# Rotary by halves: columns of the query and key weights reordered, halves exchanged out of PSUM by ScalarE, row copies issued by GpSimd

## The chip, the cores and the metric

The kernel runs on one core of one Trainium2 chip. The core has five engines that run at the same time, each with its own instruction queue, taken in order: TensorE (PE: matmuls from SBUF into PSUM), VectorE (DVE), ScalarE (ACT), GpSimd (POOL) and SyncE (SP, which here only issues DMAs). The metric is the device time of one execution in microseconds; lower is better.

## What is computed

Two layers over 512 positions of width 1024, all in float32. Each layer has a mixer of three branches (a convolution with 31 taps, a short gated convolution, a differential attention with rotary) and an MLP of width 4096, each behind an RMS norm that is modulated by a conditioning vector. The change concerns the queries and keys of the attention alone:

```python
def apply_rope(t, cos, sin):
    t1, t2 = jnp.split(t, 2, axis=-1)
    return jnp.concatenate([t1 * cos - t2 * sin, t2 * cos + t1 * sin], axis=-1)

q = apply_rope(q.reshape(bsz, seq, N_HEADS, 2, HEAD_DIM), cos, sin)
k = apply_rope(k.reshape(bsz, seq, N_HEADS, 2, HEAD_DIM), cos, sin)
...
s = jnp.einsum('bqhcd,bkhcd->bhcqk', qb, kb).astype(jnp.float32) * scale
p = jax.nn.softmax(jnp.where(mask, s, -jnp.inf), axis=-1)
a = p[:, :, 0] - lam * p[:, :, 1]
```

There are 8 heads, each with two components of 64 channels. In each component, channel i (of the first 32) and channel i + 32 are turned together. The scores of the two components go through separate softmaxes.

## The kernel before

**Numbers.** Every float32 operand of a matmul is split into a high part (rounded to TensorE's float32r type) and a low part (the rest). A product is three passes: high by high, high by low, low by high (`PASSES`, line 415). A weight chunk of 1024 x 128 is split by `w_split` (line 371): ScalarE casts the high part (line 394), one step later VectorE subtracts it from the raw weights (line 402). Raw weights come in tiles of 1024 x 256 (1 MB) on SP's queue (line 367); there are two raw tiles, so the next load is issued when a tile's second chunk has been split.

**Layout.** Activations are transposed: 128 channels on the partitions, 512 positions along the row. One `product` (line 426) is 24 matmuls of 512 columns (8 parts of the contraction, 3 passes) into one PSUM bank. For queries and keys such a product holds one head: 128 rows, component 0 in rows 0 to 63, component 1 in rows 64 to 127, and in each component the first half of the channels and then the second.

**The order of the work.** The program writes the order of all engines' instructions itself. A clock advances by one step for every 4096 columns that matmuls of the large products stream (`mm`, line 143: eight matmuls of 512 columns). Side work is written as generators: `yield n` hands back until n steps later, and `spawn` puts a generator on the heap. Whatever a generator emits lands, in that order, in the queues of its engines, behind all that was emitted before.

**A head pair.** In each layer the mixer makes four pairs of heads, each of four products (query and key of one head, query and key of the next), followed by the values of the two heads. After each of the four products `rope` (line 707) is spawned with no delay. `heads` (in `mixer`) starts head after head: each 9 steps after the one before, and not before its rotated query and key are there; the first head waits 2 more steps (`FIRST`). `attend` (line 780) then forms the scores (lines 789 and 790) in four groups, two steps apart, into two PSUM banks, each group needing the banks that the group before filled; the softmax's first VectorE instruction (line 754) empties them. Later it transposes, multiplies with the values, and forms a small norm on POOL (lines 834 to 836 and 438) whose result TensorE spreads over the rows (line 455).

**The rotation.** `rope` copies the product out of PSUM (ScalarE, line 712), and four DMAs on SP's queue copy 32 rows each, so that the tile `sw` holds every half in the place of the other (line 714). VectorE multiplies the copy by the cosines (717), `sw` by the signed sines (719), and adds (720). The sum is cast to d0 and d1 (ScalarE, 723 and 724). For the query (j even) VectorE makes the low parts e0 and e1 (728, 729); for the key it makes the low part in place (734). Then DMAs on SP's queue copy rows, 64 at a time (738, 739), so that for each component there is a tile with 128 contraction rows: for the query the high part twice and the low part twice, for the key the high part and the low part. `RWAIT` is the number of steps from those DMAs to the moment when the head may use the result.

**The start.** The first pair's four products run at the start, by quarters of the contraction while weights arrive. Their order is written out by hand in `START`: `h` casts a quarter of a weight chunk on ScalarE (line 1270), `l` subtracts on VectorE (line 1276), `m` modulates two parts of the input, `p` is a quarter of a product. p12 to p15 are the last quarters of the four products, and each spawns its `rope` (`first_product`). l13 is the low part of the weights that p13 uses; h16 and l16 split the first chunk of the values. In the second layer the first three of the four products are formed at the end of `closing`, between the halves of the layer before.

Of the kernel before, what the change touches and what calls it, by code (L numbers as in the profile page):

```python
# [43 lines left out]
CPACE, ADA0, ADA1, APACE = 0.71, 2.36, 2.19, 1.62  # L44
ADA_BR = 0
FIRST = 2
RWAIT = 2


RDELAY = (0, 1, 1)  # L50
# [21 lines left out]
def kernel(  # L72
# [31 lines left out]
    def ftile(dt=F32, shape=None):  # L104
        return slot("f", dt, shape)
# [245 lines left out]
        return s  # L351


    specs, chunks = [], []
    for l in range(L):
        for sp in wspecs(l):
            grp = sp if isinstance(sp[0], tuple) else (sp,)
            chunks += [(len(specs) + g, hh) for hh in range(2) for g in range(len(grp))]
            specs += grp
    raws, wready = [], []  # L360
# [2 lines left out]
    def raw_issue():  # L363
        if len(raws) < len(specs):
            src, c0, kk = specs[len(raws)]
            raw = wraw.tile([P, 8, 256], F32, tag="raw", name=nm("raw"))
            nc.sync.dma_start(raw[:, : abs(kk), :],
                              src[:, c0 : c0 + 256].rearrange("(k p) e -> p k e", p=P))
            raws.append(raw)

    def w_split(extra=None):


        if wnext[0] >= len(chunks):
            return
        n, hh = chunks[wnext[0]]
        wnext[0] += 1
        raw, kk = raws[n], specs[n][2]
        if kk < 0:

            shape, rs = [P, 4, 256], raw[:, 4 * hh : 4 * hh + 4, :]
            n_k = 4
        else:
            shape, rs = [P, 8, P], raw[:, :kk, hh * P : (hh + 1) * P]
            n_k = kk
        if extra:
            half = [P, n_k // 2] + shape[2:]
            his = [slot(extra, F32R, half) for _ in range(2)]
            parts = [(hf, rs[:, i * half[1] : (i + 1) * half[1], :]) for i, hf in enumerate(his)]
        else:  # L390
            hi = wpool.tile(shape, F32R, tag="wh", name=nm("wh"))
            parts = [(hi[:, :n_k, :], rs)]
        for h_, r_ in parts:
            A.copy(h_, r_)  # L394
        yield 1
        if extra:
            los = [slot(extra, F32R, half) for _ in range(2)]
        else:
            lo = wpool.tile(shape, F32R, tag="wl", name=nm("wl"))
            los = [lo[:, :n_k, :]]  # L400
        for l_, (h_, r_) in zip(los, parts):
            V.tensor_tensor(l_, r_, h_.bitcast(F32), op=ALU.subtract)  # L402
        wready.append(([h_[:, k, :] for h_, _ in parts for k in range(n_k // len(parts))],
                       [l_[:, k, :] for l_ in los for k in range(n_k // len(parts))], extra))
        if hh == 1:
            raw_issue()
# [300 lines left out]
    def rope(pp, res, j):  # L707

        t, sw = ftile(), ftile()
        A.copy(t, pp)
        for q in range(4):
            nc.sync.dma_start(sw[32 * q : 32 * q + 32, :], t[32 * (q ^ 1) : 32 * (q ^ 1) + 32, :])  # L714
        yield 1
        u = ftile()
        V.tensor_tensor(u, t, cos_t, op=ALU.mult)
        yield 2
        V.tensor_tensor(sw, sw, sin_t, op=ALU.mult)  # L719
        V.tensor_tensor(u, u, sw, op=ALU.add)  # L720
        yield 1
        d0, d1 = slot("qk", F32R), slot("qk", F32R)
        A.copy(d0, u)
        A.copy(d1[64:, :], u[64:, :])
        yield 1
        if j % 2 == 0:
            e0, e1 = slot("qk", F32R), slot("qk", F32R)
            V.tensor_tensor(e0, u, d0.bitcast(F32), op=ALU.subtract)
            V.tensor_tensor(e1[64:, :], u[64:, :], d1[64:, :].bitcast(F32), op=ALU.subtract)
            moves = ((d0, d0, d1, d1), (e0, e0, e1, e1))  # L730
            parts = (d0, d1, e0, e1)
        else:
            lo = u.bitcast(F32R)
            V.tensor_tensor(lo, u, d0.bitcast(F32), op=ALU.subtract)
            moves = ((d0, u, d1, u),)
            parts = (d0, d1)
        for a0, b0, a1, b1 in moves:
            nc.sync.dma_start(a0[64:, :].bitcast(F32), b0[:64, :].bitcast(F32))
            nc.sync.dma_start(a1[:64, :].bitcast(F32), b1[64:, :].bitcast(F32))
        yield RWAIT  # L740
        res.append(parts)

# [403 lines left out]
    def angles():  # L1146
# [15 lines left out]
        for t in (ang, n_):  # L1162
            V.tensor_scalar(out=t, in0=t, scalar1=PI, scalar2=-PI, op0=ALU.min, op1=ALU.max)
        yield
        A.activation(sin_t, ang, AF.Sin, scale=rc[:, 1:2])
        A.activation(cos_t, n_, AF.Sin)

# [97 lines left out]
    def high(n):  # L1265
        if n == 16:
            w_tasks.append(w_split("cv"))
            next(w_tasks[0])
        else:
            A.copy(w_quarter(n, 0), raw_quarter(n))  # L1270

    def low(n):
        if n == 16:
            next(w_tasks[0], None)
        else:
            V.tensor_tensor(w_quarter(n, 1), raw_quarter(n), w_quarter(n, 0).bitcast(F32), op=ALU.subtract)
            if n // 4 == 3 and n % 4 > 1:
                raw_issue()

# [98 lines left out]
```

## Time and profile before

| | |
|---|---|
| median of 3 runs | 1906.89 us (1906.71 to 1907.18) |
| the profiled execution | 1904.28 us, of which 1902.5 us is the span from the first to the last instruction |
| TensorE busy | 1874.3 us, 99% of the span |
| VectorE, ScalarE, POOL busy | 1256.0, 785.8 and 63.4 us |
| granted TensorE clock, mean | 0.997 |
| DMA | 241.20 MB, mean 127 GB/s |

Line numbers such as L714 are those of the kernel before. A group's row gives the line, the engine, the operation, the tiles it writes and reads, and the number of instructions; then the busy time, the mean duration, and how long the engine stood idle just before them and on whom. A timeline's row gives the start in the span, the duration, and in brackets the idle time before it and what ended it. Matmuls overlap, and their ends are modelled: the time from one start to the next is the better measure of TensorE. The first layer's attention runs from about 55 to 300 us, the second's from about 985 to 1215 us.

### The profile page before, as it was taken

To read this page: it belongs to the slowest core of one execution; us is meant where nothing else is said; L and a number is where in the kernel's file an instruction comes from. 1 tells how busy PE (TensorE), PEld (TensorE's weight loads), DVE (VectorE), ACT (ScalarE), POOL (GpSimd) and SP (SyncE) were. 2 spreads that over 40 slices of the span, in tenths; PEclk is the share of its full clock that TensorE was granted. 3 is DMA by queue.
4 is the path that set the end of the run, shared out by engine and by line. 5 is a ranking of instruction groups with operands and counts; after the bars stand their busy time and mean duration, and the time that the engine had idled before them with its cause. 6 is when DMAs were issued, how large, how long until landed. Compare 5 with 4: busy or idle time off the path is not lost.

```text
span 1902.5 us, 24972 instructions
## 1 busy us (share of the span) xinstructions
PE 1874.3 (99%) x9565; PEld 1599.9 (84%) x9565; DVE 1256.0 (66%) x2139; ACT 785.8 (41%) x1420; POOL 63.4 (3%) x109
## 2 busy tenths in 40 slices
PE   8999999999999999999999999999999999999998
PEld 6788888888889888888898888888888898888888
DVE  7788789996676556565677777898654563333336
ACT  4466652223333524333445666322243353424253
POOL 1011010000000000000000000000000000000000
PEclk9999999999999999999999999999999999999999
DMA  8644323444554455555535442232233422223221
GB/s 272 181 130 126 101 67 98 151 138 145 166 178 135 139 178 195 177 185 182 171 97 142 123 122 73 89 104 96 67 100 100 133 89 89 89 93 106 89 89 67
DMA packets 211527, 241.20 MB, mean 127 GB/s; under 512 B 10408, under 2 KB 178480, under 8 KB 211408
## 3 DMA queue, kind: packets, MB, share of 16 engines
q1 hardware_dynamic: 210480, 239.38, 40.6%
q8 instruction: 75, 1.23, 0.3%
q0 software_dynamic: 768, 0.23, 0.1%
q14 instruction: 44, 0.36, 0.1%
q10 hardware_dynamic: 160, 0.01, 0.0%
HBM read 216.50 MB, written 2.10 MB: 115 GB/s over the span
## 4 chain that ended last, share of the span: by engine, by line
PE 93%; DMA 3%; DVE 2%; issue 1%; SPq 1%; ACT 1%; POOL 0%; POOLq 0%; DVEq 0%; ACTq 0%
PE mm L145 83%; PE s L145 3%; DMA f<-f 2%; PE t L817 1%; PE s L789 1%; PE s L790 1%; PE t L806 1%; SPq L714 1%; PE t L1193 1%; PE t L455 0%; PE t L303 0%; PE t L825 0%; POOL st L438 0%; DVE f L719 0%; PE t L1214 0%
## 5 line engine op out<-in xcount | busy, mean ns | idle before, releaser
L145 PE MATMUL mm<-h,wh 128*128 128x512 f32 x2720 | 851.3, 392 | 0.0
L145 PEld LDWEIGHTS mm<-h,wh 128*128 128x128 f32 x2720 | 509.6, 188 | 103.3
L145 PE MATMUL mm<-h,wl 128*128 128x512 f32 x1360 | 533.6, 392 | 0.0
L394 ACT CAST wh<-raw 128x1024 fp32r<-128x1024 f32 (+1 forms) x308 | 308.9, 1005 | 407.2 <-PE mm L145 358.2
L402 DVE TENSOR_TENSOR wl<-raw,wh 128x1024 fp32r<-128x1024 f32 (+1 forms) x308 | 358.2, 1166 | 69.6 <-ACT wh L394 65.9
L145 PE MATMUL mm<-qk,wh 128*128 128x512 f32 (+1 forms) x1024 | 300.2, 376 | 0.0
L145 PEld LDWEIGHTS mm<-h,wl 128*128 128x128 f32 x1360 | 256.2, 188 | 51.9
L145 PEld LDWEIGHTS mm<-qk,wh 128*128 128x128 f32 x1024 | 188.2, 188 | 35.1
L145 PE MATMUL mm<-qk,wl 128*128 128x512 f32 (+1 forms) x512 | 192.6, 376 | 0.0
L912 DVE SCALAR_TENSOR_TENSOR cv<-v,caw,cv 128x511 f32<-128x511 f32 (+14 forms) x240 | 176.0, 733 | 4.2
L499 DVE SCALAR_TENSOR_TENSOR xT<-mm,ada,xT 128x512 f32<-128x512 f32 (+1 forms) x81 | 56.0, 691 | 151.2 <-PE mm L145 151.0
L281 DVE SCALAR_TENSOR_TENSOR araw<-araw,cact,araw 128x512 f32<-128x512 f32 x140 | 104.6, 747 | 25.2 <-DMA araw<-in_w_ada_dram 24.7
L145 PEld LDWEIGHTS mm<-qk,wl 128*128 128x128 f32 x512 | 96.3, 188 | 17.2
L1059 ACT ACTIVATE f<-mm 128x512 f32<-128x512 f32 x60 | 35.9, 598 | 160.6 <-PE mm L145 160.6
L145 PE MATMUL mm<-o,wh 128*128 128x512 f32 (+1 forms) x320 | 95.5, 381 | 0.0
L145 PE MATMUL mm<-v,wh 128*128 128x512 f32 (+1 forms) x320 | 94.9, 379 | 0.0
L145 PE MATMUL mm<-wh,h 128*128 128x256 f32 x448 | 84.1, 284 | 0.0
L761 ACT ACTIVATE cv<-cv,st 128x128 f32<-128x128 f32 (+3 forms) x128 | 71.0, 558 | 25.6 <-DVE st L754 25.2
L1033 DVE SCALAR_TENSOR_TENSOR f<-f,mm 128x512 f32<-128x512 f32 x38 | 26.1, 687 | 83.6 <-PE mm L145 83.6
L469 DVE TENSOR_TENSOR qk<-f,qk 128x512 fp32r<-128x512 f32 x38 | 26.3, 691 | 77.4 <-ACT qk L466 77.2
L438 POOL TENSOR_TENSOR st<-st,nhalf 128x4 f32<-128x4 f32 (+2 forms) x29 | 31.2, 1076 | 1368.0 <-DVE st L460 1013.4
L145 PEld LDWEIGHTS mm<-wh,h 128*128 128x128 f32 x448 | 70.8, 191 | 0.4
(259 smaller groups left out, 2282.9 us busy)
## 6 DMA issues: line engine op xcount, KB each, us to landing
raw<-in_w_in_dram SPq DMA_DIRECT2D x66, 1024.0 KB, 5.2
raw<-in_w_ff_dram SPq DMA_DIRECT2D x64, 1024.0 KB, 5.4
araw<-in_w_ada_dram SPq DMA_DIRECT2D x160, 256.0 KB, 3.0
f<-f SPq DMA_DIRECT2D x128, 64.0 KB, 2.0
qk<-qk SPq DMA_DIRECT2D x64, 128.0 KB, 2.6
raw<-in_w_c_out_dram SPq DMA_DIRECT2D x8, 1024.0 KB, 5.0
raw<-in_w_out_dram SPq DMA_DIRECT2D x8, 1024.0 KB, 5.0
qk<-in_w_ada_dram SPq DMA_DIRECT2D x16, 256.0 KB, 6.0
```

What stands on the lines that cost most here:

```text
L145: T.matmul(ps, lhsT, rhs, start=start, stop=stop)
L281: V.scalar_tensor_tensor(out=part, in0=r, scalar=cact[:, k : k + 1], in1=part, op0=ALU.mult, op1=ALU.add)
L394: A.copy(h_, r_)
L402: V.tensor_tensor(l_, r_, h_.bitcast(F32), op=ALU.subtract)
L438: G.tensor_tensor(y, v[:, :n], nhalf[:, :n], op=ALU.pow)
L469: V.tensor_tensor(lo, src, hi.bitcast(F32), op=ALU.subtract)
L499: V.scalar_tensor_tensor(out=xT[e][:, t0:t1], in0=pp[:, t0:t1], scalar=g[:, e : e + 1], in1=xT[e][:, t0:t1], op0=ALU.mult, op1=ALU.add)
L714: nc.sync.dma_start(sw[32 * q : 32 * q + 32, :], t[32 * (q ^ 1) : 32 * (q ^ 1) + 32, :])
L761: A.activation(p[cc][:, :n], p[cc][:, :n], AF.Exp, bias=nb[:, cc : cc + 1], scale=-1.0, accum_out=l0[:, i : i + 1] if cc == 0 else s1)
L912: V.scalar_tensor_tensor(out=ac[:, s:], in0=glu[j][:, : S - s], scalar=wk, in1=ac[:, s:], op0=ALU.mult, op1=ALU.add)
L1033: V.scalar_tensor_tensor(out=t, in0=t, scalar=1.0, in1=pp, op0=ALU.add, op1=ALU.mult)
L1059: A.activation(r, pp, AF.Relu)
```

## The change

1. The columns of the query and key weights are put in another order as they are split: for each head first the 32 first-half channels of component 0, those of component 1, then the second halves of both. Each cast and each subtraction of such a chunk becomes two instructions over half the columns (`turn_high`, `turn_low`), at the start too.
2. A product then holds all first halves in rows 0 to 63 and all second halves in rows 64 to 127. Two ScalarE copies of 64 rows, straight out of PSUM, put the halves in each other's place; the four exchange DMAs are gone. VectorE multiplies by the cosines straight out of PSUM, in the rope's first step.
3. The sign of the sines follows: the first 64 rows get -1, the others 1 (two small `memset`s).
4. d1 and e1 are made over all 128 rows.
5. The row copies move 32 rows at a time, twice as many of them, on GpSimd's DMA queue.
6. The waits between the rope's steps were 1, 2, 1, 1 and `RWAIT` = 2; they are 1, 1, 1 and `RWAIT` = 3.

```diff
-RWAIT = 2
+RWAIT = 3
...
-    specs, chunks = [], []
+    specs, chunks, turned = [], [], set()
     for l in range(L):
         for sp in wspecs(l):
             grp = sp if isinstance(sp[0], tuple) else (sp,)
+            if len(grp) > 1 and grp[0][1] in range(2560, 3584):
+                turned.update(range(len(specs), len(specs) + 2))
...
+    def by_half(w):
+        v = w.rearrange("p k (c s f) -> p k s c f", c=2, s=2)
+        return [v[:, :, i] for i in range(2)]
+
+    def by_part(w):
+        v = w.rearrange("p k (s c f) -> p k s c f", c=2, s=2)
+        return [v[:, :, i] for i in range(2)]
+
+    def turn_high(hi, raw):
+        for a, b in zip(by_part(hi), by_half(raw)):
+            A.copy(a, b)
+
+    def turn_low(lo, raw, hi):
+        for a, b, c_ in zip(by_part(lo), by_half(raw), by_part(hi.bitcast(F32))):
+            V.tensor_tensor(a, b, c_, op=ALU.subtract)
...
+        turn = kk > 0 and n in turned
         for h_, r_ in parts:
-            A.copy(h_, r_)
+            if turn:
+                turn_high(h_, r_)
+            else:
+                A.copy(h_, r_)
...
-            V.tensor_tensor(l_, r_, h_.bitcast(F32), op=ALU.subtract)
+            if turn:
+                turn_low(l_, r_, h_)
+            else:
+                V.tensor_tensor(l_, r_, h_.bitcast(F32), op=ALU.subtract)
...
-        t, sw = ftile(), ftile()
-        A.copy(t, pp)
-        for q in range(4):
-            nc.sync.dma_start(sw[32 * q : 32 * q + 32, :], t[32 * (q ^ 1) : 32 * (q ^ 1) + 32, :])
-        yield 1
-        u = ftile()
-        V.tensor_tensor(u, t, cos_t, op=ALU.mult)
-        yield 2
+        sw, u = ftile(), ftile()
+        A.copy(sw[:64, :], pp[64:, :])
+        A.copy(sw[64:, :], pp[:64, :])
+        V.tensor_tensor(u, pp, cos_t, op=ALU.mult)
+        yield 1
         V.tensor_tensor(sw, sw, sin_t, op=ALU.mult)
         V.tensor_tensor(u, u, sw, op=ALU.add)
         yield 1
         d0, d1 = slot("qk", F32R), slot("qk", F32R)
         A.copy(d0, u)
-        A.copy(d1[64:, :], u[64:, :])
+        A.copy(d1, u)
         yield 1
         if j % 2 == 0:
             e0, e1 = slot("qk", F32R), slot("qk", F32R)
             V.tensor_tensor(e0, u, d0.bitcast(F32), op=ALU.subtract)
-            V.tensor_tensor(e1[64:, :], u[64:, :], d1[64:, :].bitcast(F32), op=ALU.subtract)
+            V.tensor_tensor(e1, u, d1.bitcast(F32), op=ALU.subtract)
...
         for a0, b0, a1, b1 in moves:
-            nc.sync.dma_start(a0[64:, :].bitcast(F32), b0[:64, :].bitcast(F32))
-            nc.sync.dma_start(a1[:64, :].bitcast(F32), b1[64:, :].bitcast(F32))
+            for r in (0, 64):
+                G.dma_start(a0[r + 32 : r + 64, :].bitcast(F32), b0[r : r + 32, :].bitcast(F32))
+                G.dma_start(a1[r : r + 32, :].bitcast(F32), b1[r + 32 : r + 64, :].bitcast(F32))
         yield RWAIT
         res.append(parts)
...
+        V.memset(rc[:64, 1:2], -1.0)
+        V.memset(rc[64:, 1:2], 1.0)
         A.activation(sin_t, ang, AF.Sin, scale=rc[:, 1:2])
...
-            A.copy(w_quarter(n, 0), raw_quarter(n))
+            turn_high(w_quarter(n, 0), raw_quarter(n))
...
-            V.tensor_tensor(w_quarter(n, 1), raw_quarter(n), w_quarter(n, 0).bitcast(F32), op=ALU.subtract)
+            turn_low(w_quarter(n, 1), raw_quarter(n), w_quarter(n, 0))
```

## The prediction

> **What bounds the kernel now.** The page comes first: the span, the engines, and the DMA issues by kind.
>
> ```profile
> span 1902.5 us, 24972 instructions
> ...
> PE 1874.3 (99%) x9565; PEld 1599.9 (84%) x9565; DVE 1256.0 (66%) x2139; ACT 785.8 (41%) x1420; POOL 63.4 (3%) x109
> ...
> f<-f SPq DMA_DIRECT2D x128, 64.0 KB, 2.0
> ```
>
> TensorE fills 99% of the span. The change takes no matmul away, so it can only give back moments in which TensorE stands still or runs slowly, and it can only cost by making new ones. The second view is therefore TensorE's table of waits (who, on whom: total, times, longest).
>
> ```profile
> PE s L789 <- DVE st L754: 5.6, 5, 2.2
> PE s L789 <- DMA qk<-f: 3.4, 2, 3.2
> ```
>
> L789 forms the scores, so the first two rows are attention's: scores wait five times for a bank that the softmax's first VectorE instruction (L754) must empty, and twice for the keys' row copies. The 3.2 us one is layer 0's first head. The timeline of TensorE shows what it costs beyond the wait, and the table by stretches shows the granted clock there (0.91).
>
> ```profile
> 72.29 0.61 PE L145 MATMUL mm<-h,wh 128*128 128x512 f32 x2
> 76.10 0.30 PE L789 MATMUL s<-qk,qk 128*128 128x128 f32 x1 [3.19 <-DMA qk<-f]
> ...
> 77.11 0.73 PE L145 MATMUL mm<-h,wl 128*128 128x512 f32 x1
> ...
> 80.06 0.62 PE L145 MATMUL mm<-h,wh 128*128 128x512 f32 x2
> ...
> 82.13 0.28 PE L789 MATMUL s<-qk,qk 128*128 128x256 f32 x1
> ...
> 82.60 0.63 PE L145 MATMUL mm<-h,wh 128*128 128x512 f32 x2
> ```
>
> ```profile
> 60.00:80.00 20.00, 15.92 (x103) 14.39 (x102) 14.79 (x29) 10.59 (x20) 0.56 (x1) 0.91 0.63 165
> ...
> 100.00:120.00 20.00, 18.25 (x133) 16.71 (x132) 18.28 (x46) 13.52 (x30) 1.59 (x4) 1.00 0.48 126
> ```
>
> Nine matmuls lie between 80.06 and 82.13: 0.23 us each. The seven between 77.11 and 80.06 took 2.95 instead of 1.61 us, and four score matmuls took 1.01 us (76.10 to 77.11), against 0.47 for four larger ones at 82.13. So this wait cost 3.19 + 1.34 + 0.54 = 5.07 us.
>
> Why do the five others wait? The chain of waits passes, shortly before each of them, through an exchange of halves, the copy f<-f of L714:
>
> ```profile
> 91.51 5.96 DMA f<-f
> ...
> 106.11 4.63 DMA f<-f
> ...
> 1020.23 5.99 DMA f<-f
> ...
> 1067.28 6.15 DMA f<-f
> ...
> 1114.42 6.68 DMA f<-f
> ```
>
> The page's median landing is 2.0 us; these took 4.6 to 6.7, on the queue that also carries the 1 MB weight loads. VectorE takes its instructions in order: its product with the sine (L719) stands waiting for the exchange, L754 is queued behind, and TensorE waits for L754.
>
> **The change, part by part.** Unit costs, from the groups between 60 and 310 us (busy us, mean ns, then idle):
>
> ```profile
> L723 ACT CAST qk<-f 128x512 fp32r<-128x512 f32 x16 | 9.9, 621 | 12.2 <-DVE f L720 6.5 <-PE s L789 5.6
> L724 ACT CAST qk<-f 64x512 fp32r<-64x512 f32 x16 | 9.9, 618 | 0.3
> ...
> L717 DVE TENSOR_TENSOR f<-f,cos_t 128x512 f32<-128x512 f32 x14 | 9.6, 685 | 0.0
> ...
> L712 ACT COPY f<-mm 128x512 f32<-128x512 f32 x13 | 7.5, 580 | 14.3 <-PE mm L145 14.2
> ...
> L991 DVE TENSOR_TENSOR f<-f,mm 128x512 f32<-128x512 f32 x2 | 1.4, 684 | 1.0 <-PE mm L145 1.0
> ...
> L908 DVE TENSOR_SCALAR cv<-v,caw,prm 128x512 f32<-128x512 f32 x2 | 1.1, 542 | 0.0
> ...
> L994 DVE TENSOR_SCALAR f<-f,prm 128x512 f32<-128x512 f32 x2 | 1.0, 480 | 0.0
> ```
>
> 1. *The exchange goes* (128 DMAs on SP's queue). Two ScalarE copies of 64 rows out of PSUM replace one of 128. Rows do not set the price (L724 with 64 costs what L723 does with 128), so this adds one 0.58 us copy per rope on an engine that is 41% busy; d1 and e1 over all rows are free by the same two rows. The cosine product reads PSUM, which costs VectorE nothing more (L991 against L717). With no exchange to wait for, the five L754 waits have lost their cause: **gain 5.6 us**. No row shows what is late next; the bounds are 0 (something else holds VectorE equally long) and 5.6, and I take all and charge new lateness in part 5.
>
> 2. *Halved weight casts and subtractions.* VectorE's cost shows where the program already cuts a 1024-column split in two (55.09 against 57.22); ScalarE's is bounded by two casts like L723 against one of 1024 columns:
>
> ```profile
> 65.61 1.05 ACT L394 CAST wh<-raw 128x1024 fp32r<-128x1024 f32 x1 [3.54 <-DMA raw<-in_w_in_dram]
> ```
>
> ```profile
> 39.83 0.35 DVE L1183 TENSOR_SCALAR part<-v,cact 128x256 f32<-128x256 f32 x1
> ...
> 51.74 0.42 DVE L1276 TENSOR_TENSOR wl<-raw,wh 128x256 fp32r<-128x256 f32 x1
> ...
> 55.09 1.29 DVE L402 TENSOR_TENSOR cv<-raw,cv 128x512 fp32r<-128x512 f32 x2
> ...
> 57.22 1.15 DVE L402 TENSOR_TENSOR wl<-raw,wh 128x1024 fp32r<-128x1024 f32 x1
> ...
> 66.69 1.22 DVE L402 TENSOR_TENSOR wl<-raw,wh 128x1024 fp32r<-128x1024 f32 x1 [2.07 <-ACT wh L394]
> ...
> 72.53 0.69 DVE L734 TENSOR_TENSOR f<-f,qk 128x512 fp32r<-128x512 f32 x1
> ```
>
> That is +0.19 us on ScalarE (2 × 0.62 − 1.05) and +0.14 on VectorE per chunk, 2 to 3 us of each over a layer's 16 chunks, covered by their free shares. Runs of 32 columns have no row. Lower bound 0; upper bound doubled (+1.2 us per chunk on VectorE), which would feed the second rival. I take the low end, since today's casts already read runs of 128 out of rows of 256 at about one column per ns. At the start there is no such cover: between the rows at 39.83 and 51.74 VectorE's timeline has no pause, and six quarter subtractions (L1276) stand ahead of the last modulation. Six times 0.14: **loss 0.8 us**; bounds 0 and 15 × 0.14 = 2.1.
>
> 3. *The cosine product moves ahead of l13.* The start list runs "p12 l13 h16 p13". The rope's first step now puts a VectorE instruction, waiting for p12's last matmul, in front of l13, the low part of the weights of p13, whose third matmul needs it.
>
> ```profile
> 53.39 0.39 PE L145 MATMUL mm<-h,wl 128*128 128x512 f32 x1
> ...
> 54.07 0.39 PE L145 MATMUL s<-h,wl 128*128 128x512 f32 x1
> ```
>
> p12 ends at 53.8. Then 0.69 (product) and about 0.5 (l13 in halves): l13 is ready at 55.0 instead of 52.2, and p13's third matmul, at 54.07 now, waits about 1.0 us with the semaphore's way: a new wait. **Loss 1.1 us**; bounds 0.5 (l13 alone) and 1.6 (with slow running in the proportion 5.07 to 3.19).
>
> 4. *Row copies on POOL, twice as many, half as large; the head starts one step (8 matmuls, 1.85 us) earlier*, because the waits inside a rope fall from seven steps to six. What POOL's issues cost and how long such a copy takes:
>
> ```profile
> 118.92 0.53 POOL L204 DMA_DIRECT2D f<-in_b_ada_dram  x1 [16.25 <-PE t L221]
> ...
> 120.29 1.29 POOL L835 TENSOR_SCALAR st<-st 128x4 f32<-128x4 f32 x1
> ...
> 159.84 0.22 POOL L835 TENSOR_SCALAR st<-st 128x4 f32<-128x4 f32 x1
> ```
>
> ```profile
> f<-in_conv_a_w_dram POOLq DMA_DIRECT2D x2, 62.0 KB, 2.5
> ```
>
> A query rope issues 8 × 0.53 = 4.2 us, a key rope 2.1 us. Queued behind them on POOL are the head's small norm (L834 to L438) and a few parameter loads; the norm is wanted only steps later, so I charge nothing. SP loses all its rope work, and with it a block: in the start its next weight load stands behind eight exchange issues,
>
> ```profile
> 59.87 0.53 SPq L367 DMA_DIRECT2D raw<-in_w_in_dram x1
> ```
>
> lands at 65.6, and holds ScalarE's cast (65.61, 3.54 us idle) and VectorE's subtraction (66.69), with the ropes' later steps behind. In the new order, the first two ropes' casts stand ahead of that cast.
>
> The first head of layer 0, then: VectorE, from 53.8, has to do four cosine products, three pairs of sine product and sum, the query's two subtractions and the key's one (13 × 0.69 = 9.0), l13 (0.5), l16 (1.29), two more splits (2.4) and the lambda work (56.38 to 57.22: 0.84), together 14.0, with about 1 us of waiting for p13: the key's low part is ready at 68.8 instead of 73.2. Four issues (2.1), the last at 70.4, and 2.5 to land: 72.9. TensorE wants it one step before 72.9 and 1.1 later through part 3, at 72.1. So 0.8 us of wait remains, 1.0 with some slow clock. **Gain 5.07 − 1.0 = 4.1 us**. Bounds: no wait at all (5.07), and a landing late by what exchanges lost behind a weight load (5.96 against 2.0, so 4 us): a wait of 4.8 us, which with the same 1.88 of slow running costs 6.7, a loss of 1.6. I take the low landing, as POOL's rows are nearest. In layer 1 the same wait is only 0.2 us (3.4 less 3.2): nothing either way.
>
> The Trainium skill (DMA: Bandwidth & Descriptors, section SWDGE vs HWDGE vs iDMA) states that DMAs from GpSimd and from SP feed different queues inside each DMA engine, which serves them in turn. By it the copies would not stand behind a weight load; by the slow f<-f rows they would, and the sum would be 1.1 instead of 6.8 us. No run so far shows a POOL copy beside such a load.
>
> 5. *VectorE meets TensorE at each product's end*, where it used to come a step later and wait for nothing newer than a copy. Bounds: 0, and 0.69 us at each of the 36 places where scores are formed while later ropes run (two layers, six heads, three groups after the first), 25 us. I take **1.0 us of loss**, near 0, since L717's row shows no idle time and VectorE is busy 66% of the span.
>
> Sum: 5.6 + 4.1 − 0.8 − 1.1 − 1.0 = 6.8 us. The profiled execution would go from a span of 1902.5 to 1895.7; its own time of 1904.28 lies 2.6 below the median, 1906.89, which becomes **1900.1**.
>
> **The rivals.**
>
> *First: the first score is as late as ever.* The copies collide with weight loads (the far bound in part 4): 6.8 − 5.7 = 1.1 us of gain, **1905.8**, no change to be measured. For it: the new due time is earlier and the exchange did suffer so. Against: VectorE's 4.4 us.
>
> *Second: VectorE, tied to product ends, is late for the softmax.* Place: L754, the same row that has 5.6 us now. Price: at 0.4 us on each of the 36 places, 14.4 instead of 1.0; the sum becomes −6.6, **1913.5**. It breaks even at about 0.22 us a place and decides (0.2% slower) from 0.32. For it: in-order queues and a fuller VectorE. Against: no L754 wait in the trace without an exchange before it.
>
> *Third: POOL's issues are held up by VectorE.* POOL's L835 took 0.22 us, or 1.29 when held. With 1.07 more on each of the twelve issues of a first query and key, both layers' first heads are 12.8 us later: 6.8 − 25, **1925**; slower from 0.45 us an issue. Against: POOL's issue at 118.92 took 0.53 in a stretch (100 to 120 us) where VectorE was busy for 18.28 of 20 us.
> The Trainium skill (SBUF — State Buffer, section Who interferes with whom) states that GpSimd cannot write descriptors while VectorE runs a copy or scalar instruction in a two-port mode. The groups above show only four such instructions (L908, L994) in 250 us, so by it too this stays rare here.
>
> *Fourth: more comes back*, since SP's earlier weight loads also shorten waits of ScalarE and VectorE: no new lateness, no wait at the first head, 1906.9 − 5.6 − 5.07 + 1.9 = **1898**, or less.
>
> **How the numbers follow.** Forecast 0.55, first rival 0.21, second 0.09, third 0.05, fourth 0.10. The forecast's own range is 1897 to 1903.5. The range of 1894.5 to 1908.5 leaves out most of the second and third rivals and a little below the fourth. A measurement of this kernel can tell 0.2% (3.8 us) from no change: faster means below 1903.1. Nearly all of the forecast and the fourth case lie there: 0.65. Same: the first rival and the forecast's tail, 0.22. Slower: second and third, 0.13.
>
> **What the changed profile would show.** Right: no f<-f issues; the waits of L789 on L754 under 1.5 us in all; the wait at layer 0's first score under 1.5 us, its clock back near 1.00; a new wait of about 1 us near 54 us, inside p13; POOL's issues near 0.53 us. Wrong: key copies landing 5 us after issue (first rival); L754 waits many and small (second); POOL's issues above 0.9 us (third); halved L402 rows well over 0.7 us each.

## The result, and the profile after

The changed kernel is slower: 1927.66 us median of 4 runs (1924.84 to 1930.09) against 1907.04 for the kernel before on the same chip, a ratio of 1.0114 (95% interval 1.0099 to 1.0128). The prediction was 1900.1. The profiled execution took 1930.09 us, with a span of 1928.3. One execution further below, of experiment 10, took 2682.76 us at a granted clock of 0.655; it is a slow run, and no ratio here uses it.

The page of the changed kernel shows the span, the engines and the DMA issues; the exchange f<-f is gone, and POOL, at 63.4 us before, is busy for 159.8:

```profile
span 1928.3 us, 25012 instructions
...
PE 1883.2 (98%) x9565; PEld 1605.5 (83%) x9565; DVE 1255.7 (65%) x2187; ACT 805.2 (42%) x1498; POOL 159.8 (8%) x301
...
qk<-qk POOLq DMA_DIRECT2D x128, 64.0 KB, 4.2
...
qk<-f POOLq DMA_DIRECT2D x64, 64.0 KB, 1.9
```

Lines have moved: the two ScalarE copies out of PSUM are L739 and L740, the cosine product L741, sine product and sum L743 and L744, the row copies L763 and L764, the softmax's first instruction L779, the scores L814 and L815, the halved subtraction L388, the small norm L859 to L464 and the transposes that need it L481. TensorE's table of waits in the changed kernel (us in all, times, longest):

```profile
PE t L481 <- POOL st L464: 8.0, 5, 3.7
...
PE s L814 <- DVE st L779: 4.1, 6, 1.0
PE t L251 <- DVE st L246: 3.4, 1, 3.4
PE s L814 <- DMA qk<-f: 3.4, 1, 3.4
PE t L1230 <- ACT f L1326: 2.5, 1, 2.5
...
PE s L145 <- DVE wl L388: 2.0, 1, 2.0
```

Of the two waits that the change was to remove, the softmax's is smaller (5.6 before), and the row copies' has moved from layer 0's first head to layer 1's. The other four rows are new or larger (the norm's, L481, has its row of the kernel before further below; L251 had 0.8). Three places are looked at here, and the end of the program is a fourth; at L251, near 74 us, TensorE waits for VectorE, which is late by then.

*The start.* Timeline of the changed kernel, all engines, in order of time:

```profile
29.62 1.53 DVE L1213 SCALAR_TENSOR_TENSOR part<-o,cact,part 128x256 f32<-128x256 f32 x3
...
31.60 0.06 DVE L1191 MEMSET rc<- 64x1 f32 x1
31.69 0.72 ACT L1192 ACTIVATE sin_t<-at,rc 128x512 f32<-128x512 f32 x1 [2.96 <-DVE rc L1191]
...
32.84 0.56 ACT L1326 COPY f<-t 128x512 f32<-128x512 f32 x1
...
33.45 1.12 PE L1230 MATMUL t<-ident,f 128*128 128x128 f32 x4 [2.52 <-ACT f L1326]
```

The change sets the sine's signs by two memsets of 0.06 us on VectorE. In VectorE's queue they stand behind the products of the first modulation, so ScalarE's sine waits 2.96 us; the copy L1326 is queued behind it, and TensorE waits for that copy.

*The rope's first step.* The same view, at the first rope:

```profile
56.35 0.61 PE L145 MATMUL s<-h,wh 128*128 128x512 f32 x2
56.60 0.58 ACT L739 COPY f<-mm 64x512 f32<-64x512 f32 x1 [2.97 <-PE mm L145]
57.20 0.58 ACT L740 COPY f<-mm 64x512 f32<-64x512 f32 x1
...
57.81 0.69 DVE L741 TENSOR_TENSOR f<-mm,cos_t 128x512 f32<-128x512 f32 x1 [3.39 <-ACT f L740]
58.41 0.48 DVE L388 TENSOR_TENSOR wl<-raw,wh 128x128 fp32r<-128x128 f32 x2
...
58.96 0.50 PE L145 MATMUL s<-h,wl 128*128 128x512 f32 x1 [1.99 <-DVE wl L388]
```

The product's inputs are there when the first copy starts, at 56.60. It starts at 57.81, 0.03 us after the second copy is over, though it reads nothing that these copies write: both read the same PSUM bank. VectorE's table of waits has this 19 times in the changed kernel (first row). In the kernel before, the product waited twice for the copy that it did read (second row):

```profile
DVE f L741 <- ACT f L740: 37.5, 19, 3.5
```

```profile
DVE f L717 <- ACT f L712: 5.2, 2, 2.9
```

Behind the product stand the low weights of p13 (L388, "l13"), and TensorE waits 1.99 us for them.

*A norm behind row copies.* POOL's and TensorE's timeline in layer 0:

```profile
144.61 0.50 POOL L763 DMA_DIRECT2D qk<-qk  x1 [22.34 <-DVE qk L752]
...
148.39 0.50 POOL L764 DMA_DIRECT2D qk<-qk  x1
151.29 0.51 POOL L204 DMA_DIRECT2D f<-in_b_ada_dram  x1 [2.40 <-DMA qk<-qk]
...
152.33 0.55 POOL L859 TENSOR_TENSOR st<-st 128x4 f32<-128x4 f32 x1
...
153.57 1.05 POOL L464 TENSOR_TENSOR st<-st,nhalf 128x4 f32<-128x4 f32 x1
...
154.68 0.65 PE L481 MATMUL t<-ident,st 128*128 128x128 f32 x4 [3.72 <-POOL st L464]
```

A query's eight copies first wait for VectorE's low part (L752), take eight issues (to 148.89), and the next DMA may not be issued before the first copy has landed at 151.01, 6.41 us after its issue (it signals by the semaphore of that first copy: the program has eight for POOL's queue). The norm stands behind all that. In the kernel before, the row of the norm's wait was:

```profile
PE t L455 <- POOL st L438: 2.8, 3, 0.9
```

*The end.* POOL's last DRAIN, by the source view of the program's last line (times in ns: shortest, median, longest), in the changed kernel and then in the kernel before:

```profile
L1400 POOLq DRAIN  x3: 40/102/8532, 1919.0 to 1928.0; - x3
```

```profile
L1373 POOLq DRAIN  x3: 40/106/2734, 1897.2 to 1902.2; - x3
```

In the kernel before, POOL's 2.73 us are over while SP still waits for the last output. In the changed kernel they are 8.53 us. SP is done at 1923.49, and POOL's next event is at 1927.57: 4.1 us in which nothing runs.

Compared matmul by matmul, the changed kernel is 8.8 us behind where the kernel before is at 88.8 us, 13.7 at 161.6, 17.2 from 272 to 987 (no rope runs there), 21.8 at the last matmul, and 25.8 at the end of the span. Waits are only a part of it. The table by stretches of the changed kernel shows a granted clock of 0.76, where the kernel before has 0.91:

```profile
60.00:80.00 20.00, 16.61 (x90) 14.97 (x89) 16.39 (x32) 12.10 (x21) 8.01 (x17) 0.76 0.54 152
```

In shorter stretches the clock is either 1.00 or 0.50. Up to the last matmul it is 0.50 in six stretches of the changed kernel, 27.2 us in all, and in two of the kernel before, 6.8 us. Each of the six begins during one of TensorE's waits of 1.0 to 3.7 us, or at most 1.3 us after it. Two of the six, and then one of the kernel before:

```profile
60.20:63.60 3.40, 3.40 (x9) 2.18 (x8) 2.17 (x5) 2.30 (x4) 0.00 (x0) 0.50 0.89 290
73.80:80.60 6.80, 6.65 (x31) 6.66 (x32) 5.67 (x11) 1.89 (x4) 4.99 (x11) 0.50 0.47 103
```

```profile
76.50:79.90 3.40, 3.27 (x10) 2.70 (x10) 0.62 (x5) 0.99 (x4) 0.00 (x0) 0.50 0.80 190
```

As an estimate from these figures, a TensorE that is busy all the while loses half of such a stretch: up to 13.6 us in the changed kernel, against 3.4. Its waits, without the two at the program's start that both kernels have, are 25.4 us against 12.6. Together that is 23 us more, near the 21.8 found at the last matmul.

### The profile page after: what moved, and what is told of

Same layout as the page of the kernel before. It is cut to its first block, busy times and chain, and to the rows that moved or that the text cites. A ratio compares the mean times of both kernels' runs of the same rounds, so it can differ in the third digit from the quotient of the medians.

```text
span 1928.3 us, 25012 instructions
## 1 busy us (share of the span) xinstructions
PE 1883.2 (98%) x9565; PEld 1605.5 (83%) x9565; DVE 1255.7 (65%) x2187; ACT 805.2 (42%) x1498; POOL 159.8 (8%) x301
## 4 chain that ended last, share of the span: by engine, by line
PE 90%; DVE 3%; DMA 3%; issue 2%; POOL 1%; ACT 1%; SPq 0%; POOLq 0%; ACTq 0%; DVEq 0%
PE mm L145 81%; PE s L145 3%; PE t L842 1%; PE s L814 1%; DMA qk<-qk 1%; PE s L815 1%; PE t L831 1%; DMA qk<-in_w_ada_dram 1%; PE t L481 1%; POOL st L464 0%; DVE wl L388 0%; PE t L303 0%; PE t L850 0%; DMA raw<-in_w_in_dram 0%; POOL qk L764 0%
## 5 line engine op out<-in xcount | busy, mean ns | idle before, releaser
L417 ACT CAST wh<-raw 128x1024 fp32r<-128x1024 f32 (+1 forms) x282 | 282.1, 1001 | 400.3 <-PE mm L145 357.7
L428 DVE TENSOR_TENSOR wl<-raw,wh 128x1024 fp32r<-128x1024 f32 (+1 forms) x282 | 326.6, 1160 | 52.2 <-ACT wh L417 49.3
L464 POOL TENSOR_TENSOR st<-st,nhalf 128x4 f32<-128x4 f32 (+2 forms) x29 | 32.1, 1107 | 1371.0 <-DVE st L486 1016.3
L779 DVE CUSTOM_DVE_ANT_0 cv<-s,mask 128x128 f32<-128x128 f32 (+3 forms) x128 | 57.4, 485 | 42.7 <-PE s L815 38.5
```

The source lines that it names most:

```text
L464: G.tensor_tensor(y, v[:, :n], nhalf[:, :n], op=ALU.pow)
L779: V.tensor_tensor_reduce(out=pp[:, :n], in0=sps[cc][:, :n], in1=mask[:, S - n :], op0=ALU.add, op1=ALU.min, scale=-0.125, scalar=3.0e38, a ...
```

## The experiments

Three theories stood at first. A: these are separate losses, each from an engine's in-order queue, and they add up. B: most of it is the row copies on POOL's queue. C: most of it is the cosine product's wait at its PSUM bank, which makes VectorE late for everything.

All edits below are to the changed kernel, unless said otherwise. Kernels ran in three groups, each beside the kernel before (medians 1906.88, 1905.47 and 1906.12), so groups are compared by ratios; 0.001 is 1.9 us, and an interval is some 0.0010 to 0.0020 to either side. A difference of two ratios is uncertain by some 0.0015 to 0.0020.

**1. Memsets early.**

```
         V.tensor_copy(ang, posi)
+        V.memset(rc[:64, 1:2], -1.0)
+        V.memset(rc[64:, 1:2], 1.0)
...
-        V.memset(rc[:64, 1:2], -1.0)
-        V.memset(rc[64:, 1:2], 1.0)
```

> The changed kernel with the two memsets of the sines' sign moved up to VectorE's first step of the angles, where VectorE has time. Changed kernel: 1927.7 us. Theory A (the loss is a sum of separate in-order waits; in the changed trace the memsets stand behind VectorE's partial products, ScalarE's sine waits 2.96 us for them, and TensorE 2.52 us for the copy queued behind the sine): about 4 us less, 1922 to 1925. Theory B (the row copies on GpSimd's queue carry the loss) and theory C (the cosine product, which takes its turn at the PSUM bank behind ScalarE's two copies, makes VectorE late everywhere): no change, 1926 to 1929.

Measured: 1923.56, ratio 1.0088 (1.0073 to 1.0103); the wait of L1230 is gone. So two memsets in the wrong place cost some 4 to 5 us, a difference of 0.0026 that is just clear of its uncertainty.

**2. l13 ahead of p12.**

```
-    "... p10 p12 l13 h16 p13 l16 p14 p15"
+    "... p10 l13 p12 h16 p13 l16 p14 p15"
```

> The changed kernel with l13 written ahead of p12 in the start list, so that no cosine product stands between VectorE and the weights of p13. The changed trace shows TensorE waiting 1.99 us there. Theory A: 2 to 3 us less than 1927.7, 1924 to 1926, the 1.99 us wait gone. Theories B and C: under 1.5 us less, because the time is lost again behind the later waits.

Measured: 1927.04, ratio 1.0107 (1.0092 to 1.0122), not told from the changed kernel. The 1.99 us are gone and come back one step later, as this kernel's waits show:

```profile
PE t L251 <- DVE st L246: 4.2, 1, 4.2
...
PE mm L145 <- DVE cv L428: 1.4, 1, 1.4
...
PE mm L145 <- DVE wl L428: 0.9, 1, 0.9
```

VectorE as a whole is late there; changing its order only changes who waits.

**3. Cosine product one step later**, still out of PSUM.

```
         A.copy(sw[64:, :], pp[:64, :])
-        V.tensor_tensor(u, pp, cos_t, op=ALU.mult)
         yield 1
+        V.tensor_tensor(u, pp, cos_t, op=ALU.mult)
```

> The changed kernel with the cosine product (still out of PSUM) one step later, after the rope's first pause, so that VectorE no longer stands waiting for TensorE's product and ScalarE's two copies (37.5 us in 19 waits in the changed trace). It also passes l13 in the order, so that wait goes too. Theory A: 4 to 8 us less, 1920 to 1924. Theory C: 15 us less or more, 1913 or below. Theory B: under 3 us less.

Measured: 1912.79, ratio 1.0032 (1.0021 to 1.0042), 14.9 us below the changed kernel: theory C's number, and more than A allowed. The l13 wait is gone without moving l13, and L779's falls to 1.3. The norm's wait stays (7.2).

**4. Row copies on SP.**

```
-                G.dma_start(...)
+                nc.sync.dma_start(...)
```

> The changed kernel with the row copies (32 rows each, as many) issued by SyncE as before the change. Takes away POOL's issues ahead of the head's norm: in the changed trace TensorE waits 3.7 and 1.4 us for that norm in layer 0, and 3.4 us for a key copy in layer 1. Theory A: 6 to 10 us less than 1927.7, 1918 to 1922, the first two waits gone. Theory B: 15 us less or more, 1913 or below. Theory C: under 4 us less.

Measured: 1913.15, ratio 1.0027 (1.0015 to 1.0039), 14.5 us below. The norm's wait is as before the change (2.9, 3 times), and POOL's last DRAIN is back at 2.73 us. So B has a share as large as C's. Whether two cures of 15 us each cure one loss twice was the next question.

**5. Three edits together** (1, 2 and 3; copies on POOL).

> Three edits together, on the changed kernel: memsets of the sine's scale early, l13 ahead of p12 in the start list, cosine product after the rope's first yield. Row copies stay on POOL. Sum of what the three gave alone: 1927.7 - 14.9 (cosine product later) - 4.1 (memsets) - 0.6 (l13) = 1908.1. If the start's two edits only work where VectorE is late (rival: one lateness, cured once), nothing comes on top of the cosine product: 1912 to 1913. Either way the end stays long, for POOL still has its 192 row copies: its last drain near 8.5 us, closing about 4 us after SP's.

Measured: 1909.0, ratio 1.0018 (1.0009 to 1.0028), against 1.0032 with the product's edit alone. The start's edits add to it, by some 3 of the 4.7 us expected (0.0014, about as much as its uncertainty).

**6. Four edits together** (1 to 4).

> As the kernel with three edits, and the row copies on SP's queue. Theory 'independent losses': 1927.7 - 14.9 - 14.5 - 4.1 - 0.6 = 1893.6. Theory 'shared loss' (the norm on POOL waits behind row copies only because VectorE, late by its turn at the PSUM bank, hands the copies over late; either cure takes most of it): against the three edits, only the end's 4.1 us and the norm's remaining excess of 4.3 us (7.2 against 2.9) go: 1899.7. Theory 'SP's queue is as bad' (row copies land late beside the weight loads, the first score of layer 0 waits 3 us again and runs at a lower clock): 1904 or more. POOL's drain 2.7 us in each case.

Measured: 1896.09, ratio 0.9946 (0.9931 to 0.9961): faster than the kernel before, by about 10 us, and between the two theories' figures. The losses are nearly independent. TensorE's waits in this kernel:

```profile
PE t L481 <- POOL st L464: 3.1, 3, 1.1
...
PE t L251 <- DVE st L246: 2.2, 1, 2.2
PE s L814 <- DVE st L779: 1.3, 2, 1.0
PE mm L145 <- DVE wl L428: 0.5, 1, 0.5
```

There is no wait for a row copy left, though SP issues them among the weight loads, and the exchange's 5.6 us are down to 1.3. Against experiment 5 only the queue differs, and the spans differ by 12.8 us: matmul by matmul, 4.3 go at the norm near 140 us (with a clock of 0.50 for 3.4 us behind it), 4.3 more before layer 1's first scores, 4.0 after the last matmul; 1.6 lost near 187 us and 1.5 won near 70 us about cancel. The second of these is seen in POOL's timeline of experiment 5:

```profile
993.43 0.50 POOL L764 DMA_DIRECT2D qk<-qk  x1
1000.30 0.50 POOL L763 DMA_DIRECT2D qk<-f  x1 [6.37 <-PE mm L145]
```

and SP's timeline of this kernel:

```profile
992.37 0.51 SPq L763 DMA_DIRECT2D qk<-f  x1
```

The key's low part was ready at 996.82 and 992.34, so POOL's copy stood 3.5 us, for a signal of TensorE's, and SP's did not. In the traces, POOL's copy waits for three semaphores, of an earlier DMA, of VectorE and of TensorE (this one is set at 999.77); SP's copy waits for two, of an earlier DMA and of VectorE.

Moving a DMA to another queue changed what it waits for.

**7. A third of the copies on POOL**: as 5, but POOL issues only the high parts of the queries.

```
+        for q_, (a0, b0, a1, b1) in zip((G if j % 2 == 0 else nc.sync, nc.sync), moves):
...
-                G.dma_start(...)
+                q_.dma_start(...)
```

> As the kernel with three edits, but of the 192 row copies only the 64 for the high parts of the queries are issued by POOL, the other 128 by SP. The drain theory says that POOL's last drain grows with the DMAs that POOL has issued: 2.73 us for 24 and 8.53 us for 216 make 0.0302 us for each, so 4.67 us for 88, and the program closes within 0.3 us of SP's own last drain. Rival (the drain is long as soon as the rows of the copies go through POOL at all, or it waits for something else at the end): 8.5 us again. Time: 'shared loss' puts it at 1900 to 1903, since POOL then issues 4 copies of 0.5 us for a query instead of 8 and never has more than four in flight.

Measured: 1898.95, ratio 0.9960 (0.9945 to 0.9974). Up to the last matmul it runs like experiment 6 (8.2 us ahead of the kernel before, against 8.1): four copies at a time on POOL cost nothing. The end does:

```profile
L1400 POOLq DRAIN  x3: 40/102/7959, 1889.0 to 1897.4; - x3
```

7.96 us for 88 DMAs is neither the 4.67 of the linear theory nor the rival's 8.53. The DMA issues of this kernel also compare the two queues, SP with the low parts and POOL with the high parts of the same queries:

```profile
qk<-qk SPq DMA_DIRECT2D x64, 64.0 KB, 5.9
qk<-qk POOLq DMA_DIRECT2D x64, 64.0 KB, 5.7
```

**8. Cosine product ahead of the copies**, otherwise as 6.

```
+        V.tensor_tensor(u, pp, cos_t, op=ALU.mult)
         A.copy(sw[:64, :], pp[64:, :])
         A.copy(sw[64:, :], pp[:64, :])
-        V.tensor_tensor(u, pp, cos_t, op=ALU.mult)
         yield 1
```

> As the kernel with four edits, but the cosine product stands ahead of the two ScalarE copies in the rope's first step, instead of a step later: VectorE has the first turn at the PSUM bank and ScalarE waits 0.69 us. Theory 'turn at the bank' (the 1.17 us that VectorE stands waiting for two ScalarE copies is the loss): VectorE then starts at the product's end, and the time is within 2 us of the four edits. Theory 'tied to the product's end' (any VectorE instruction that waits for TensorE's last matmul holds up what is queued behind it): as with the row copies on SP alone, less the start's two edits: 1913.2 - 4.7 = 1908.5.

**9. Cosine product behind the copies, in the same step** (as the change has it), otherwise as 6.

> As the kernel with four edits, but the cosine product where the change has it, in the rope's first step behind the two ScalarE copies (so: memsets early, l13 ahead of p12, row copies on SP). It differs from the kernel with the product ahead of the copies in nothing but who reads the PSUM bank first. Theory 'turn at the bank': each L741 stands 1.17 us longer, 1906 to 1909 (sum of single edits: 1913.2 - 4.7 = 1908.5). Theory 'tied to the product's end': the order of the two readers matters little, within 2 us of the product-first kernel's 1901.4.

Measured: 1901.39, ratio 0.9975 (0.9965 to 0.9985), with the product first; 1909.93, ratio 1.0020 (1.0011 to 1.0030), with the copies first; 0.9946 for experiment 6, with the product a step later. So of 0.0074 (14 us), 0.0045 (8.6 us) hang on nothing but who reads the bank first, and 0.0029 (5.5 us) are left when the product still stands at TensorE's end but reads first. Both theories have a share, the turn the larger one. With the product first, it is ScalarE that waits, at less cost; that wait is part of the 5.5 us too. Its table of waits (here L739 is the product and L740 the first copy):

```profile
ACT f L740 <- DVE f L739: 42.0, 26, 4.0
```

When the order is reversed, so is the wait. Product and copies write different tiles, and all they have in common is the bank that they read; the turn at the bank is what is waited for.

Of the 4.1 us by which the last matmul of the product-first kernel's profiled execution is behind experiment 6's, all arise in layer 1, where the scores wait for L779 three times for some 0.95 us (at 1023.58, 1070.22 and 1117.71), against once in experiment 6, and the transposes L831 once for 1.5. This smaller part is what the second rival described.

Where the turn's 8.6 us lie: the two profiled executions' spans are 10.2 us apart (1898.5 and 1908.7), and 5.3 of these have arisen before layer 0's first scores. The same stretch, product first and then copies first (the sixth column after the engines' times, before the DMA share, is the granted clock):

```profile
60.00:80.00 20.00, 16.96 (x117) 15.83 (x118) 14.83 (x34) 11.20 (x23) 0.56 (x1) 1.00 0.49 131
```

```profile
60.00:80.00 20.00, 14.78 (x103) 14.31 (x103) 14.83 (x34) 10.02 (x18) 0.56 (x1) 0.83 0.42 116
```

**10. The kernel before, with its row copies on POOL** and nothing else.

```
-            nc.sync.dma_start(...)
+            G.dma_start(...)
```

> The kernel before, with its 96 row copies (64 rows each) issued by POOL instead of SP, and nothing else. Theory 'POOL's queue costs by itself': POOL's last drain near 8.1 us (120 DMAs, between the 7.96 us seen for 88 and the 8.53 for 216), so the program closes about 3.6 us after SP, and the norm (L438) stands behind copies that wait for VectorE: 1910.5 to 1915. Rival 'SP's relief pays' (weight loads and exchanges no longer stand behind copies that wait): the end's 3.6 us are earned back, 1905 to 1908.

Measured: 1909.74, 1918.28 and 1918.26, ratio 1.0066 (1.0046 to 1.0086); two of the three lie above what either theory expected, and the other lies between the two. Only the one of 1909.74 was profiled. In it the norm's wait hardly grows (3.1, 4 times, against 2.8), the softmax's does (7.9 against 5.6), the last matmul comes 0.6 us earlier than before, and the end is 6.1 us longer:

```profile
L1373 POOLq DRAIN  x3: 40/93/10576, 1896.6 to 1907.7; - x3
```

So in this execution, with half as many issues and VectorE in time, POOL's queue costs only the end. For the other two that is not shown. 10.58 us for 120 DMAs, 96 of them of 64 rows, is again off the expected 8.1. Why the other two took 8.5 us more stays open; their granted clocks were 0.993 and 0.994, against 0.997.

**11. 32 copies on POOL**, otherwise as 6.

```
+        for q_, (a0, b0, a1, b1) in zip((G if j % 2 == 0 and len(pooled) < 8 and not pooled.append(j) else nc.sync, nc.sync), moves):
```

> As the kernel with four edits, but 32 row copies, those for the high parts of layer 0's eight queries, on POOL: 56 DMAs in all on POOL's queue. Three drains are known: 2.73 us for 24, 7.96 for 88, 8.53 for 216. If the drain grows with the count up to some 90 and then hardly: 2.73 + 32 x (7.96 - 2.73)/64 = 5.3 us. If it looks only at what was issued lately (layer 0's copies are over a millisecond old at the end): 2.7 us. If any row copy makes it long: 7.9 us.

Measured: 1896.59, ratio 0.9949 (0.9931 to 0.9967), and

```profile
L1400 POOLq DRAIN  x3: 40/102/5347, 1887.8 to 1893.7; - x3
```

5.35 us against 5.3 expected. From 24 to 88 DMAs the drain grows by 0.082 us for each copy of 32 rows, and 32 copies of layer 0 count though they are over a millisecond old; from 88 to 216 it hardly grows (8.53). What ends the growth, and why copies of 64 rows bring more, stays open.

**12. Weight splits whole**, otherwise as 6.

```
-        for a, b in zip(by_part(hi), by_half(raw)):
-            A.copy(a, b)
+        A.copy(hi, raw)
...
-        for a, b, c_ in zip(by_part(lo), by_half(raw), by_part(hi.bitcast(F32))):
-            V.tensor_tensor(a, b, c_, op=ALU.subtract)
+        V.tensor_tensor(lo, raw, hi.bitcast(F32), op=ALU.subtract)
```

> As the kernel with four edits, but the weight chunks of queries and keys are cast and subtracted whole instead of in halves; their columns then stay in the old order, so the kernel computes other queries and keys: the reordering of the rotary columns is what it leaves out. Prediction's own figure: 0.8 us in the start, and nothing later, where free shares of ScalarE and VectorE cover 0.19 and 0.14 us a chunk: 1895 to 1896. Rival (VectorE's lateness is what every loss here had in common, so the halves are not covered either): 1891 to 1893.

Measured: 1895.76, ratio 0.9946 (0.9931 to 0.9961), a span of 1894.0 against 1894.4: the halves cost nothing that can be seen.

## Why the prediction was wrong

The balance first. From the changed kernel (1.0114) to the four edits (0.9946) are 0.0168, 32 us. The parts, each from two kernels that differ in it alone: the product's place 0.0074, POOL's queue 0.0072, the memsets 0.0026, l13 0.0007; together 0.0179, equal within the intervals. Without these four (and so with the row copies on SP), the change gives 10 us, near the 5.6 + 4.1 = 9.7 of the forecast's gains. Their sum was about right; four costs were missed or far too small. Of the waits' price, the forecast counted slow running only at the first head and in the bounds; by the estimate above it is up to 10 of the 21.8 us lost at the last matmul.

*Part 1, the exchange goes.* The gain was nearly right once the product stood a step later: the L754 row of 5.6 us is 1.3 in experiment 6, but still 4.1 in the changed kernel. The step that failed is "the cosine product reads PSUM, which costs VectorE nothing more (L991 against L717)". Its duration is the same indeed, 0.69 us at 57.81. But two durations were compared where a wait was at stake: in the kernel before, the product read a ScalarE copy in SBUF, and now VectorE and ScalarE want the same bank at the same moment. The copy "on an engine that is 41% busy" was called free; the product stands behind both copies, 1.2 us. In the trace the product waits for a semaphore of TensorE and for one of ScalarE, which L740 sets at its end.

The Trainium skill (PSUM — Partial Sum Buffer, section PSUM bank collisions raise a hardware error) states that two engines may not access one bank and the same quarter of its partitions at once, reads against reads included, and that software has to keep them apart. The timeline shows this program keeping them apart: 0.03 us lie between L740's end and L741's start. No run here shows what an overlap would do.

*Part 5, VectorE meets TensorE at each product's end.* Charged with 1.0 us between bounds of 0 and 25, "near 0, since L717's row shows no idle time and VectorE is busy 66% of the span". The product's place was worth 14 us. This is the largest term that was mis-sized. L717's idle row, taken from 60 to 310 us, spoke for an instruction that waited for something long done; it says nothing of the same instruction placed where its input is the newest thing in the program. And a mean share of 66% says little of the ropes' stretches, where VectorE was busy for 16.39 of 20 us (60 to 80 us of the changed kernel). The second rival had the price nearly right (14.4), but by luck: its price was 0.4 us at each of 36 softmax places. L779's wait didn't grow against the kernel before (4.1 against 5.6), and about half of the turn's price lies before the first softmax (5.3 of 10.2 us between the profiled executions of experiments 8 and 9). Only the smaller part, with the product first, lies where it said.

*Part 3.* A new wait of 1.1 us inside p13 was forecast; it is 1.99, as l13 stood behind 1.2 us of copies too. Taking it away gave 0.6 us, which is within the noise: it was one face of a late VectorE.

*Part 2.* 0.8 us was charged, and experiment 12 finds nothing; the lower end of the bounds was right. Two halves of a chunk take 1.28 us where the whole took 1.15, as estimated (0.14 more):

```profile
140.62 1.28 DVE L388 TENSOR_TENSOR wl<-raw,wh 128x512 fp32r<-128x512 f32 x2
```

*Part 4, the copies.* POOL's issues took 0.50 us (0.53 forecast), so the third rival falls, though its 1925 lies nearest to what was measured. (The rows shown for it held four copies or scalar instructions of VectorE; between 60 and 310 us the trace has twelve, 3.8 us in all.) Layer 0's first score has no wait, and the first head's gain of 4.1 us was there: between the same matmuls the changed kernel wins back 5.7. Three things failed. First, "the norm is wanted only steps later, so I charge nothing": the cover was gone where eight issues stood ahead of it, the first of them waiting for VectorE; with four issues (3.4 us of waits in experiment 7, 3.1 in experiment 10's profiled execution) the norm is nearly as early as before, while with eight it waits 7.0 us even if VectorE is in time (experiment 5). Second, in layer 1 the key's copies "nothing either way" waited 3.4 us, on a signal that SP's copies don't need. Third, no step looked at the program's end.

The landing was taken as 2.5 us, "as POOL's rows are nearest". The slow f<-f rows were nearer. In the chain of waits of the changed kernel,

```profile
144.61 6.41 DMA qk<-qk
```

and the trace has the weight load issued by SP at 141.94 landing at 150.83, the eight POOL copies then between 151.01 and 152.31. The rule of the Trainium skill that the prediction cited (DMA: Bandwidth & Descriptors, section SWDGE vs HWDGE vs iDMA), queues served in turn, was taken to let such small copies by; here they landed right behind the load. The first of their packets runs at 147.17, 2.56 us after the issue (1.1 at the first head), and until 149.98 packets of both queues run; whether these take turns isn't shown. Nor was POOL's queue the faster one for the same copies: their median landing was 4.0 us in experiment 5 and 4.0 on SP's queue in experiment 6. It did no harm at the first head, where no load was in the way.

*Not in the prediction at all:* the two memsets (4 to 5 us), of which the change's text shows the place. Their cost was not their 0.06 us but the queue that they joined.

*What the changed profile would show.* Right: no f<-f issues, no wait at layer 0's first score, issues near 0.53, halves of weights at about 0.6 us each. Wrong: L789's waits on L754, 4.1 instead of under 1.5, the wait inside p13 (1.99 instead of about 1), and the clock (0.76 instead of near 1.00 between 60 and 80 us).

## What to carry to other kernels

Before an operand is moved from SBUF to PSUM, ask who else reads that bank at that moment: in this kernel the second reader paid the first one's whole time (1.2 us for two copies), and it was 8.6 us cheaper to let the engine with the fuller queue read first, and cheaper still to let it read a step later. Of every instruction that is added or moved to another queue, however short, write down what stands ahead of it there and what it newly waits for; a share of busy time says nothing about that. Count with a wait also the slow running behind it. And look at the end of the program as well: a queue that was hardly used before may have to be wound up.

## What was not expected of the hardware

- GpSimd's last DRAIN was longer, the more copies of 32 rows GpSimd had issued: 2.73 us for 24 DMAs (parameter loads alone), 5.35 for 56, 7.96 for 88, 8.53 for 216. With 96 copies of 64 rows, 120 DMAs, it was 10.58, so the count alone doesn't set it. At the end of the changed kernel it left 4.1 us in which nothing ran.
- A ninth DMA on POOL's queue stood 2.40 us until the first of eight in flight had landed (151.29 in the changed kernel's timeline). That is the program's doing: its DMAs on that queue take eight semaphores in turn.
- Copies of 64 KB, issued by POOL, landed right behind a 1 MB load from SP's queue, the first of them 6.41 us after its issue; at the first head of layer 0, with no load in the way, it was 1.9 us.
- TensorE's granted clock falls to 0.50 for 3.4 or 6.8 us at a time, near waits of 1.0 us and more, so a wait can cost more than it lasts: between 60 and 80 us it was 0.76 in the changed kernel, 0.91 in experiment 6, 0.83 in experiment 9 and 1.00 in experiment 8. But the same wait of 2.2 us at L251 is followed by such a stretch in experiment 6 (at 67.6 us) and by none in experiment 8. What the clock follows wasn't tested.
